# Turning u and spreading the S5 tables with SBUF-to-SBUF DMAs in a one-core S5 and sparse-attention trunk

## The chip, the core and the metric

The kernel runs on one core of a Trainium2 chip. The metric is the device time of one execution in microseconds (us), from the first to the last instruction and a little around it. Five engines work side by side, each in its own order of instructions: TensorE (PE, the matmuls; PEld are its weight loads), VectorE (DVE), ScalarE (ACT), GpSimd (POOL) and SyncE (SP, which issues nearly all loads here). SP, ACT and POOL can each issue DMAs, and all of these run on the core's 16 DMA engines.

## The reference, cut to what matters

The model is a two-layer decoder trunk on 256 positions of width 2048 in float32. Layer 0 is a diagonal state-space mixer (S5), layer 1 is sparse attention; between them one shared set of keys and values is projected. Every sub-layer is normalised and modulated by vectors that come from c (shift, scale, gate). Around the change only this part counts:

```python
u, z = jnp.split(h @ w_in, 2, axis=-1)
ug = u.reshape(B_, L, SSM_GROUPS, SSM_GROUP)          # 128 groups of 16 channels
bu = jnp.einsum('blgc,gnc->blgn', ug, bb)             # per group: 16 channels -> 64 states
x  = associative_scan(a, bu)                          # over the 256 positions, complex
y  = einsum('blgn,gcn->blgc', x, c) + d_skip * ug     # per group: 64 states -> 16 channels
y  = gelu(y); y = y * sigmoid(y @ w_glu + b_glu)
out = (y * silu(z)) @ w_out
```

The modulation vectors are products of silu(c) with large weights (`mod_w`, `kv_mod_w`); "a modulation block" below means 128 of their outputs, 1 MiB of weights.

## The kernel before, in words

All large projections are done block by block (128 output channels, 1 MiB of weights). A block is loaded in two halves of 512 KB into a ring of eight raw buffers (`raw_tile`, L95). `split_w` (L195) turns each raw buffer into a rounded part `hi` (ACT, L203) and a rest `lo` (DVE, L204), and `project_half` (L223) multiplies them with the activations in three matmuls for each of eight slices of 128 inputs (L228 to L230), 24 matmuls for a half. A raw buffer is free again when DVE is done with it, so a late DVE holds up the loads, which are issued in order on SP.

The modulation blocks are done in one of two ways. `dve_mod` (L138, "d") loads a block as two raw buffers and multiplies and sums each against silu(c) with one DVE instruction (L145). `pe_mod_pair` (L150, "m") does two blocks on TensorE (L158, L163). `NA` and `NB` (L40) say how many blocks go to TensorE: 18 here, with 78 on DVE.

u is projected in two parts. Its first eight blocks are computed row by row in `u_rows` (L289), while the normalised input h is still being made. The other eight blocks are "u" halves, and the sixteen blocks of z are "z" halves (`u_half` L567, `z_half` L578), which are placed by hand. `PLAN` (L59) is a list of strings, one for each call of `fill()` (L593): a letter is a half of u or z, a modulation block (d) or pair (m), or a piece of the later stages (c, q). Calls of `fill()` stand between the steps of the S5 scan, so the strings set which projection work stands beside which step. A scheduler in the compiler then orders each engine's instructions by its own estimate of when they are ready, with the order of the program as priority.

The S5 part works on two halves f of the groups (eight blocks each). For each of them:

- `u_out` (L544) evicts a block of u from PSUM into the tile x0. `u_turn(f)` (L547) then brings the channels of a group and four sub-sequences j of positions together on the partitions: for each of four g, eight matmuls with columns of a selection matrix `pick` (L556), and one eviction by ACT (L558).
- `scan_in(f)` (L598): 128 small matmuls of u with the input tables, evicted by ACT (L615, L616), with four calls of `fill()`.
- `scan_run(f)` (L627): the scan over time on DVE (L634 to L656).
- `scan_local(f)` (L658): the part of y that comes from the same short stretch of positions. Its tables (`kdt`, made at L485 to L491) are first spread into `tz`: for each of two g2 and two hl, four matmuls with a selection matrix `sel` (L668) and one eviction by ACT (L670). Then come the products tp (L676, weights from `tz`) and their eviction (L678), with one `fill()` for each g2.
- `scan_out(f)` (L681): the products of states and output tables (L692), added to U on DVE (L697), with two calls of `fill()`.
- `y_turn(f)` (L702): the way back to channels on partitions (L708), with gelu on the eviction (L711); then `y_split`.

The order is scan_in, scan_run and scan_local of half 0, two calls of `fill()`, u_turn(1), scan_in(1), scan_out(0), scan_run(1), scan_local(1), y_turn(0), y_split(0), `fill()`, scan_out(1), y_turn(1), y_split(1), `fill()`, and then the rest of z with the d's and m's of one string of the plan (L717 to L744). The glu projection (L747), w_out (L763), the norm, the projections for keys and values (w_kv) with the first rows of q, and the attention follow, with more strings. `q_rows` (L888) runs extra d's itself if the modulation blocks that a row of q needs have not been done yet (L899).

POOL issues few DMAs: the tables at the start, the row of silu(c) (`cact`, L534) and the second half's output tables (L624).

## Time and profile before

| what | value |
|---|---|
| time, median of three runs (lowest to highest) | 1359.1 us (1358.23 to 1368.98) |
| profiled execution, its own device time | 1356.18 us |
| its span, first to last instruction | 1354.5 us |
| mean granted TensorE clock | 0.971 |
| TensorE busy | 1267.1 us (94%) |
| VectorE busy | 1056.9 us (78%) |
| ScalarE busy | 688.1 us (51%) |
| GpSimd busy | 21.7 us (2%) |
| DMA traffic | 331.05 MB, mean 244 GB/s |

Busy time is the union of an engine's instructions, so matmuls that overlap count once. A granted clock of 1.0 is the higher of TensorE's two levels. The DMA share is the mean busy share of the 16 DMA engines in a stretch. "Idle before" is the time that an engine sat still just before a group's instructions, with what ended most of it.

### The profile page before, as it was taken

To read this page: it belongs to the slowest core of one execution; us is meant where nothing else is said; L and a number is where in the kernel's file an instruction comes from. 1 tells how busy PE (TensorE), PEld (TensorE's weight loads), DVE (VectorE), ACT (ScalarE), POOL (GpSimd) and SP (SyncE) were. 2 spreads that over 40 slices of the span, in tenths; PEclk is the share of its full clock that TensorE was granted. 3 is DMA by queue.
4 is the path that set the end of the run, shared out by engine and by line. 5 is a ranking of instruction groups with operands and counts; after the bars stand their busy time and mean duration, and the time that the engine had idled before them with its cause. 6 is when DMAs were issued, how large, how long until landed. Compare 5 with 4: busy or idle time off the path is not lost.

```text
span 1354.5 us, 31620 instructions
## 1 busy us (share of the span) xinstructions
PE 1267.1 (94%) x12526; PEld 1203.9 (89%) x12526; DVE 1056.9 (78%) x2291; ACT 688.1 (51%) x1463; POOL 21.7 (2%) x47
## 2 busy tenths in 40 slices
PE   2799999999889999998999899999999999999995
PEld 1678888888789999997999899999999999999995
DVE  5999769799768787659997878777888777776665
ACT  3345543437435555445455445555555565555653
POOL 2000000000100000000000000000000000000001
PEclk9899998999899999997999999999999999999998
DMA  9799954545879899869998789876555444444541
GB/s 342 259 384 316 350 194 147 212 138 197 295 280 362 299 344 327 309 232 385 322 352 272 241 278 326 273 253 216 175 199 192 149 154 145 154 143 154 187 157 62
DMA packets 93253, 331.05 MB, mean 244 GB/s; under 512 B 12512, under 2 KB 12672, under 8 KB 92080
## 3 DMA queue, kind: packets, MB, share of 16 engines
q1 hardware_dynamic: 91792, 321.45, 67.8%
q0 software_dynamic: 1312, 7.58, 1.5%
q8 instruction: 98, 1.61, 0.5%
q14 instruction: 51, 0.42, 0.1%
HBM read 324.79 MB, written 4.19 MB: 243 GB/s over the span
## 4 chain that ended last, share of the span: by engine, by line
PE 62%; DMA 4%; DVE 3%; issue 1%; ACT 1%; DVEq 0%; ACTq 0%
PE acc L230 18%; PE acc L229 18%; PE acc L228 18%; DMA raw<-in_mt_dram 3%; PE s L1002 1%; DVE lo L204 1%; PE op L1053 1%; PE macc L158 1%; PE op L1050 1%; DMA raw<-in_w_kv_dram 1%; DVE raw L145 1%; PE op L1054 1%; PE cp L838 0%; PE qacc L915 0%; PE cp L839 0%
## 5 line engine op out<-in xcount | busy, mean ns | idle before, releaser
L203 ACT ACTIVATE hi<-raw 128x512 fp32r<-128x512 f32 x640 | 400.0, 630 | 450.7 <-PE acc L229 388.6
L204 DVE TENSOR_TENSOR lo<-raw,hi 128x512 fp32r<-128x512 f32 x640 | 433.2, 688 | 154.5 <-ACT hi L203 148.2
L229 PE MATMUL acc<-hq,hi 128*128 128x256 f32 x960 | 274.6, 286 | 0.0
L228 PE MATMUL acc<-hq,hi 128*128 128x256 f32 x960 | 273.1, 285 | 0.4 <-ACT hi L203 0.4
L230 PE MATMUL acc<-hq,lo 128*128 128x256 f32 x960 | 271.0, 284 | 1.5 <-DVE lo L204 1.3
L145 DVE SCALAR_TENSOR_TENSOR raw<-raw,ey 128x1024 f32<-128x1024 f32 x156 | 189.9, 1220 | 63.0 <-DMA raw<-in_mt_dram 57.3
L229 PEld LDWEIGHTS acc<-hq,hi 128*128 128x128 f32 x960 | 181.0, 189 | 3.7 <-issue 3.3
L230 PEld LDWEIGHTS acc<-hq,lo 128*128 128x128 f32 x960 | 180.4, 189 | 3.5 <-DVE lo L204 2.1
L228 PEld LDWEIGHTS acc<-hq,hi 128*128 128x128 f32 x960 | 181.0, 189 | 1.2 <-issue 0.7
L230 PE MATMUL acc<-h,lo 128*128 128x256 f32 x384 | 112.3, 294 | 9.4 <-DVE lo L204 9.3
L230 PE MATMUL acc<-hkv,lo 128*128 128x256 f32 x384 | 112.3, 293 | 4.5 <-DVE lo L204 4.3
L228 PE MATMUL acc<-hkv,hi 128*128 128x256 f32 x384 | 112.0, 292 | 0.9 <-ACT hi L203 0.9
L228 PE MATMUL acc<-h,hi 128*128 128x256 f32 x384 | 112.8, 294 | 0.0
L229 PE MATMUL acc<-hkv,hi 128*128 128x256 f32 x384 | 111.0, 289 | 0.0
L229 PE MATMUL acc<-h,hi 128*128 128x256 f32 x384 | 110.2, 287 | 0.0
L230 PEld LDWEIGHTS acc<-h,lo 128*128 128x128 f32 x384 | 74.5, 195 | 12.4 <-DVE lo L204 11.4
L230 PEld LDWEIGHTS acc<-hkv,lo 128*128 128x128 f32 x384 | 76.1, 198 | 6.1 <-DVE lo L204 5.8
L158 PE MATMUL macc<-mraw,cz 128*32 128x128 f32 x1600 | 56.5, 292 | 24.4 <-DMA mraw<-in_m0n_dram 19.8
L228 PEld LDWEIGHTS acc<-hkv,hi 128*128 128x128 f32 x384 | 76.4, 199 | 1.5 <-ACT hi L203 1.5
L228 PEld LDWEIGHTS acc<-h,hi 128*128 128x128 f32 x384 | 74.6, 194 | 2.9 <-issue 0.8
L229 PEld LDWEIGHTS acc<-hkv,hi 128*128 128x128 f32 x384 | 76.4, 199 | 0.0
L229 PEld LDWEIGHTS acc<-h,hi 128*128 128x128 f32 x384 | 74.7, 195 | 0.0
(339 smaller groups left out, 2808.3 us busy)
## 6 DMA issues: line engine op xcount, KB each, us to landing
raw<-in_mt_dram SPq DMA_DIRECT2D x156, 512.0 KB, 5.8
raw<-in_w_z_dram SPq DMA_DIRECT2D x96, 512.0 KB, 3.8
mraw<-in_m0n_dram SPq DMA_DIRECT2D x64, 512.0 KB, 8.0
raw<-in_w_in_dram SPq DMA_DIRECT2D x48, 512.0 KB, 5.3
raw<-in_w_kv_dram SPq DMA_DIRECT2D x48, 512.0 KB, 6.2
mraw<-in_mn_dram SPq DMA_DIRECT2D x36, 512.0 KB, 6.1
raw<-in_w_glu_dram SPq DMA_DIRECT2D x32, 512.0 KB, 6.6
raw<-in_w_out_dram SPq DMA_DIRECT2D x32, 512.0 KB, 5.9
```

What stands on the lines that cost most here:

```text
L145: nc.vector.scalar_tensor_tensor(out=rf, in0=rf, scalar=1.0, in1=cact[:, 1024 * e:1024 * e + 1024], op0=OP.mult, op1=OP.mult, accum_out=mo ...
L158: nc.tensor.matmul(acc[32 * j:32 * j + 32, 128 * e:128 * e + 128], cz[:, q, :], r[:, q % 8, :], start=(e == 0 and q < 4), stop=(q >= 12), ...
L203: nc.scalar.activation(hi[:, 0:c, :], rr, AF.Copy)
L204: nc.vector.tensor_sub(lo[:, 0:c, :], rr, hi[:, 0:c, :].bitcast(F32))
L228: nc.tensor.matmul(acc, hi[:, kk, :], act(0, k), start=(k == 0), stop=False)
L229: nc.tensor.matmul(acc, hi[:, kk, :], act(1, k), start=False, stop=False)
L230: nc.tensor.matmul(acc, lo[:, kk, :], act(0, k), start=False, stop=(k == KT - 1))
L1002: nc.tensor.matmul(sp, qo(a, h)[:, qs], kk[:, kv, b, o:o + w], start=(i == 0), stop=(i == 2))
L1050: nc.tensor.matmul(op_, vc[0:15, kv, :], tcm[0:15, :], start=True, stop=True)
L1053: nc.tensor.matmul(op_, vt[:, kv, br - 1, 0, :], t[:, 0:256], start=True, stop=False)
L1054: nc.tensor.matmul(op_[:, 128:256], vt[:, kv, br - 1, 1, :], t[:, 256:384], start=False, stop=True)
```

## The change

u_turn becomes 32 DMAs for each half, each of 16 partitions with rows of 2 KB, half of them issued by ACT and half by POOL. The spread tables are written by DMAs from `kdt` into `tz`, in sets of 16 issued by POOL (`load_tz`), after `tz` has been set to zero once. The matrices `pick` and `sel` go, with their matmuls and evictions. U, the copy of u and the tables get an order of elements in which each DMA row is contiguous, so other steps read or write through other views, and the making of `kdt` has one ACT instruction more. TensorE gets 16 modulation blocks and DVE 80, and the plan is rewritten up to the keys and values: slot 0 now stands before scan_in(0), and a slot stands right behind u_turn(1).

```diff
-NA, NB = 10, 8
+NA, NB = 12, 4
 PLAN = [
-    "ud", "ud", "ud", "ud", "uu", "uu", "uuuud", "uuuudd", "zd", "z", "zd", "z", "z", "z", "zz", "zz",
-    "zz", "zz", "zz", "zz", "zz", "d", "d", "d", "", "d", "", "d", "zzzzzzddddddmm",
-    "d", "", "d", "d", "", "d", "d", "", "d", "d", "m", "d", "d", "", "d", "d",
-    "d", "m", "d", "", "d", "d", "", "m", "d", "", "d", "", "d", "", "", "",
-    "mmmm",
+    "uduudu", "u", "u", "u", "u", "uuuu", "uu", "uu", "zzzz", "z", "z", "z", "z", "z", "z", "zzzz", "zz",
+    "z", "z", "z", "z", "zz", "d", "d", "d", "", "d", "", "d", "zzzzddddm",
+    "d", "d", "d", "d", "m", "d", "d", "d", "d", "d", "m", "d", "d", "d", "d", "m",
+    "d", "d", "d", "d", "m", "d", "d", "d", "d", "m", "d", "d", "d", "", "d", "",
+    "mm",
     "d", "d", "d", "d", "dcd", "dc", "cd", "dcd", "cd", "cd", "cd",
...
-    kdt = [t.rearrange("p (m n) -> p m n", m=8) for t in kdt]
+    kdt = [t.rearrange("p (d n m) -> p d n m", d=4, m=8) for t in kdt]
...
-        nc.scalar.activation(kx, kp[:, :, 0], AF.Copy, scale=par[:, 0:1])
-        V.scalar_tensor_tensor(kx, in0=kp[:, :, 1], scalar=par[:, 1:2], in1=kx, op0=OP.mult, op1=OP.add)
+        nc.scalar.activation(kx, kp[:, :, 0].rearrange("p x (d c) -> p x d c", d=4), AF.Copy, scale=par[:, 0:1])
+        k1 = tk("k1").rearrange("p (x d c) -> p x d c", x=4, d=4)
+        nc.scalar.activation(k1, kp[:, :, 1].rearrange("p x (d c) -> p x d c", d=4), AF.Copy, scale=par[:, 1:2])
+        V.tensor_add(kx, kx, k1)
...
-    U = pool.tile([128, KT, 4, 64], F32, tag="uu", name="U")
+    U = pool.tile([128, 2, 4, 8, 64], F32, tag="uu", name="U")
...
+    nc.gpsimd.memset(tz, 0.0)
+
+    def load_tz(f, g2):
+        for hl in range(2):
+            for e in range(2):
+                i = 64 * g2 + 32 * hl + 16 * e
+                for j in range(4):
+                    o = 64 * e + 16 * j
+                    nc.gpsimd.dma_start(tz[o:o + 16, hl, j:4], kdt[f][i:i + 16, 0:4 - j])
     powers()
+    load_tz(0, 0)
     nc.gpsimd.dma_start(cact, crow.to_broadcast((128, D)))
...
         for g in range(4):
-            p = psb([128, 8, 64], "ut")
             for j in range(4):
                 for e in range(2):
-                    o = 64 * e + 32 * (j // 2)
-                    i = 32 * (2 * g + e) + (0 if j % 2 else 16)
-                    nc.tensor.matmul(p[o:o + 32].rearrange("p m (i s) -> p m i s", i=8), pick[:, i:i + 32], ucm[:, bs, :, j, :], start=(j % 2 == 0), stop=(j % 2 == 1),
-                                     skip_group_check=True)
-            nc.scalar.activation(U[:, bs, g, :], p, AF.Copy)
+                    o = 64 * e + 16 * j
+                    (nc.gpsimd if e else nc.scalar).dma_start(U[o:o + 16, f, g], ucm[f][32 * g + 16 * e:32 * g + 16 * e + 16, j])
...
         for g2 in range(2):
-            for hl in range(2):
-                pr = slice(64 * g2 + 32 * hl, 64 * g2 + 32 * hl + 32)
-                p = psb([128, 8, 4, 16], "tzp")
-                for j in range(4):
-                    nc.tensor.matmul(p[:, :, j:4, :], sel[pr, 48 - 16 * j:176 - 16 * j], kt[pr, :, 0:4 - j, :],
-                                     start=(j == 0), stop=(j == 3), skip_group_check=True)
-                nc.scalar.activation(tz[:, hl], p.rearrange("p m j c -> p m (j c)"), AF.Copy)
             for hl in range(2):
                 p = psb([128, 8, 64], "tp")
                 for m in range(8):
                     for e in range(2):
                         pr = slice(64 * e, 64 * e + 64)
-                        nc.tensor.matmul(p[pr, m, :], tz[pr, hl, m, :], U[pr, 8 * f + m, 2 * g2 + hl, :],
+                        nc.tensor.matmul(p[pr, m, :], tz[pr, hl].rearrange("p d n m -> p (d n) m")[:, :, m], U[pr, f, 2 * g2 + hl, m, :],
                                          start=(m == 0), stop=True, skip_group_check=True)
-                nc.scalar.activation(U[:, bs, 2 * g2 + hl, :], p, AF.Copy)
+                nc.scalar.activation(U[:, f, 2 * g2 + hl], p, AF.Copy)
+            if 2 * f + g2 < 3:
+                load_tz(f + g2, 1 - g2)
             fill()
...
+    fill()
     scan_in(0)
     scan_run(0)
     scan_local(0)
     fill()
-    fill()
     while ustate[0] < 2 * (16 - NR):
         u_half()
     u_turn(1)
+    fill()
     scan_in(1)
```

## Rows read from the trace of the kernel before

**Rows 1.** The page's first part: engine, busy us, share of the span, instructions.

```profile
PE 1267.1 (94%) x12526; PEld 1203.9 (89%) x12526; DVE 1056.9 (78%) x2291; ACT 688.1 (51%) x1463; POOL 21.7 (2%) x47
```

**Rows 2.** Stretches: S5 part, glu and w_out, keys and values, attention.

```profile
core 0: us, PE busy (x) PEld busy (x) DVE busy (x) ACT busy (x) POOL busy (x), PEclk, DMA share, GB/s
164.00:412.00 248.00, 234.50 (x3011) 207.81 (x3010) 200.97 (x367) 115.74 (x219) 4.64 (x15) 0.96 0.61 214
412.00:624.00 212.00, 205.44 (x2016) 200.23 (x2014) 160.56 (x300) 109.90 (x211) 0.00 (x0) 0.98 0.88 314
624.00:836.00 212.00, 202.85 (x1620) 198.69 (x1621) 181.74 (x362) 108.37 (x212) 0.00 (x0) 0.96 0.87 304
836.00:1247.00 411.00, 409.16 (x3315) 398.51 (x3314) 312.92 (x844) 226.64 (x559) 0.00 (x0) 1.00 0.56 189
```

**Rows 3.** Shorter stretches of the same view: glu, the last m's, keys and values.

```profile
412.00:507.00 95.00, 94.90 (x835) 94.06 (x834) 78.64 (x144) 52.89 (x99) 0.00 (x0) 1.00 0.92 331
605.00:624.00 19.00, 13.12 (x275) 9.99 (x273) 14.03 (x35) 9.71 (x26) 0.00 (x0) 0.82 0.89 323
624.00:730.00 106.00, 104.61 (x836) 102.05 (x837) 98.51 (x194) 55.47 (x104) 0.00 (x0) 0.95 0.94 341
730.00:836.00 106.00, 98.24 (x786) 96.64 (x785) 83.23 (x169) 52.91 (x108) 0.00 (x0) 0.97 0.79 266
```

**Rows 4.** Stretches, tile ut alone (PE, PEld, ACT busy): the two turns of u.

```profile
166.00:174.00 8.00, 7.10 (x64) 2.19 (x64) 2.32 (x4) 1.00 0.91 275
245.00:254.00 9.00, 7.10 (x64) 2.19 (x64) 2.38 (x4) 1.00 0.79 306
```

**Rows 5.** Stretches, tile tzp alone (PE, PEld, ACT busy): the tables' spread.

```profile
188.00:212.00 24.00, 8.06 (x32) 4.93 (x32) 2.39 (x4) 0.86 0.35 115
283.00:306.00 23.00, 8.06 (x32) 4.93 (x32) 2.39 (x4) 0.93 0.47 165
```

**Rows 6.** Timeline of PE (start us, us): two slices of a projection in steady state.

```profile
243.65 0.28 PE L228 MATMUL acc<-h,hi 128*128 128x256 f32 x1
...
244.01 0.28 PE L228 MATMUL acc<-h,hi 128*128 128x256 f32 x1
```

**Rows 7.** Timeline of POOL: issues of DMAs.

```profile
4.59 3.62 POOL L416 DMA_DIRECT2D stab<-in_dvec_dram  x4
...
282.32 1.06 POOL L624 DMA_DIRECT2D ct<-ctd  x2 [137.66 <-issue]
```

**Rows 8.** DMA issues: KB each, median us from issue to landing.

```profile
stab<-in_dvec_dram POOLq DMA_DIRECT2D x4, 2.0 KB, 13.2
...
l<-in_b2row_dram POOLq DMA_DIRECT2D x1, 0.5 KB, 1.7
```

**Rows 9.** Timeline of SP: one issue that waits for nothing.

```profile
163.15 0.33 SPq L191 DMA_DIRECT2D raw<-in_w_in_dram  x1
```

**Rows 10.** Timeline of DVE: the tables' end, scan_run(0)'s first and last, scan_run(1)'s first.

```profile
163.04 0.22 DVE L491 TENSOR_TENSOR ey<-ey,dg 128x64 f32<-128x64 f32 x1
...
187.90 0.69 DVE L634 TENSOR_TENSOR scr<-Vva,stab 128x512 f32<-128x512 f32 x1 [1.73 <-ACT Vva L615]
...
257.09 1.08 DVE L656 TENSOR_TENSOR Vva<-Vva,scr 128x896 f32<-128x896 f32 x1
...
269.43 0.69 DVE L634 TENSOR_TENSOR scr<-Vvb,stab 128x512 f32<-128x512 f32 x1 [1.72 <-ACT Vvb L615]
```

**Rows 11.** Timeline of ACT: the last eviction of y_turn(1).

```profile
366.28 0.60 ACT L711 ACTIVATE U<-yt 128x512 f32<-128x512 f32 x1 [0.35 <-PE yt L708]
```

**Rows 12.** Groups by line, 164 to 412 us: xcount, busy us, mean ns, idle before.

```profile
L676 PEld LDWEIGHTS tp<-U,scr 64*64 64x64 f32 x256 | 9.3, 156 | 0.8 <-issue 0.7
...
L558 ACT ACTIVATE U<-ut 128x512 f32<-128x512 f32 x8 | 4.8, 597 | 9.8 <-PE ut L556 9.8
```

**Rows 13.** The page's fifth part: a modulation half on DVE.

```profile
L145 DVE SCALAR_TENSOR_TENSOR raw<-raw,ey 128x1024 f32<-128x1024 f32 x156 | 189.9, 1220 | 63.0 <-DMA raw<-in_mt_dram 57.3
```

More of the change, by code (lines that the diff above doesn't have):

```diff
@@ L219, in split @@
     def split(act, k, src):
-        nc.scalar.activation(act(0, k), src, AF.Copy)
-        nc.vector.tensor_sub(act(1, k), src, act(0, k).bitcast(F32))
+        hi, lo = act(0, k), act(1, k)
+        if len(src.shape) == 3:
+            hi, lo = [t.rearrange("p (a b) -> p a b", a=src.shape[1]) for t in (hi, lo)]
+        nc.scalar.activation(hi, src, AF.Copy)
+        nc.vector.tensor_sub(lo, src, hi.bitcast(F32))
     def project_half(src, act, half, acc):
@@ L499, in trunk_kernel @@
             nc.scalar.activation(VH[:, :, hq_].rearrange("p r h b m -> p h r (b m)"), p, AF.Copy)
-    ucm = x0.rearrange("p m (i j s) -> p m i j s", i=8, j=4)
-    U = pool.tile([128, KT, 4, 64], F32, tag="uu", name="U")
+    ucm = [x0[:, 8 * f:8 * f + 8, :].rearrange("p a b -> p (a b)").rearrange("p (j m k) -> p j m k", j=4, m=8) for f in range(2)]
+    U = pool.tile([128, 2, 4, 8, 64], F32, tag="uu", name="U")
     scr = pool.tile([128, 4096], F32, tag="cb", name="scr")
@@ L511, in trunk_kernel @@
     w1, w2_ = [scr[:, 192 * i:192 * i + 192] for i in range(2)]
-    tz = scr[:, 2944:3968].rearrange("p (l m n) -> p l m n", l=2, m=8)
+    tz = scr[:, 2944:3968].rearrange("p (l d n m) -> p l d n m", l=2, d=4, m=8)
     def powers():
@@ L702, in y_turn @@
     def y_turn(f):
-        for mp in range(4 * f, 4 * f + 4):
+        for mp in range(4):
             p = psb([128, 2, 8, 4, 8], "yt")
@@ L714, in y_split @@
         for m in range(8 * f, 8 * f + 8):
-            split(yhl, m, ycm[:, m].rearrange("p j k -> p (j k)"))
+            split(yhl, m, ycm[:, f, :, m - 8 * f, :])
+    fill()
     scan_in(0)
```

30 lines of the change are left out of this document (11 added, 19 removed).

## The prediction

> **What bounds the kernel now.** I read the page's first part first: TensorE is busy 94% of the span and no other engine over 78% [rows 1]. Then I cut the span into stretches to see where that holds [rows 2]. In the S5 stretch (164 to 412 us) PE is busy 234.5 of 248 us while the DMA engines are at 0.61 and DVE at 201: time comes off here if PE's work does. From 412 to 836 us PE is busy 408 of 424 us, but the DMA engines stand at 0.88 and 0.87, and in single stretches at 0.92 and 0.94 with 331 and 341 GB/s [rows 2, 3]: PE and DMA are nearly level, and what is moved there can cost. The attention (836 to 1247 us) has its DMA engines at 0.56 and PE full; the change leaves its blocks alone, so I carry it over unchanged.
>
> **The change, part by part.** The sum is made against the profiled execution's own 1356.2 us (span 1354.5 and 1.7 around it); the median of the runs shown is 1359.1, so 2.9 is added at the end.
>
> *The turn of u.* Two turns, each 32 matmuls in 64 instructions, 7.10 us of PE each [rows 4]. PE is full in both places and the next step, scan_in, needs their result, so all of it was on the path: -14.2 us.
>
> *The spread of the tables.* Per half 16 matmuls in 32 instructions, 8.06 us of PE [rows 5], with DVE as full as PE around them. What makes me count them on PE: after the scan's last step PE still has z halves to do up to 412 us (chain, below). -16.1 us, so -30.3 with the turn.
>
> *What the DMAs cost.* A set of 16 on POOL: issues one behind the other took 1.06 us for two, 0.53 each [rows 7], so 8.5 us, and the last one's data come 1.7 us after its issue as for the small load there [rows 8]: 10.2 us. ACT's 16 issues at SP's 0.33 each take 5.3 us [rows 9]. What covers a set: four halves of a projection. Eight slices of three matmuls at 0.36 us a slice [rows 6] are 2.9 us for a half, 11.5 us for four. The plan puts "uuuu" behind load_tz(0,1), "zzzz" behind load_tz(1,1) and behind u_turn(1): 10.2 under 11.5, nothing exposed. load_tz(1,0) is issued some 50 us before its use. The first turn is different: POOL does load_tz(0,0) first, from the tables' end at 163.0 us [rows 10], so its share of the turn is issued from 171.5 to 180 and lands at 182, while slot 0's cover, begun at about 163, ends near 175. Exposed 7 us if PE waits, none if the scheduler brings the u's of slots 1 to 4 forward. I take +4. The bounds: 0, and with 0.9 us an issue and 13.2 to landing, as for the four small table loads whose rows are single elements [rows 7, 8], 27.7 us for a set; I stay with the nearer rows because every row here is 512 bytes or more.
>
> *ACT.* It loses 8 evictions of the turn [rows 12] and 8 like them of the spread, 9.6 us, and gains 32 issues at 0.33, 10.6 us, and four small ones for `kdt`. Busy 116 of 248 us [rows 2], so the exchange is hidden; a set of 5.3 us in front of the `hi` splits is about two halves, as long as the split buffers last. Taken as 0; without that cover up to 5 us for two turns.
>
> *Strided views.* The tp products load weights from every eighth element. No row shows such a load; the loads were busy 9.3 us for both halves [rows 12]. Between 0 and a doubling, +9; taken as 0, as in the contiguous row, since the number of loads and columns is the same. The views that ACT and DVE write through: 0, by the slack of both in rows 2.
>
> *Modulation blocks moved.* Counting the plan's letters, 20 blocks on DVE and 2 pairs on PE stood before the glu, now 11 and 1. So 7 more are loaded in glu, w_out and the "mm" behind them (16+11+2 block loads with weights, 16+7+4 and x, and 8, against 16+13+6, 16+12+4 and x, and 4), and 4 more with keys, values and q. At 1.05 MB a block: 314 GB/s times 212 us is 66.6 MB, with 7.3 more 73.9; at the 341 GB/s of the best stretch [rows 3] that takes 216.7 us, +4.7. One PE pair fewer (2.3 us of PE) stands in this stretch, where DMA sets the length, and counts nothing. For the four in the next stretch there is room in total (0.79 at its end, 22 us idle) but q_rows now has to force five d's in its last three rows, one before: 3.1 us each at 341 GB/s, 12 us for the four, if nothing covers; I take +3. Bounds: 0 and +12. DVE: 7 blocks at two times 1.22 us [rows 13], 17 us, leave the stretch of the first scan, 10 us into the last one, which had 30 us free.
>
> *TensorE's clock.* The granted clock is a mean of 0.86 where the spread of half 0 stands and 0.93 for half 1 [rows 5]: part of the time at the lower level. Work lost: 0.14 of 24 and 0.07 of 23 us, 5 us. It may come back with these matmuls gone, or a wait for a DMA may take as much. Taken as 0; bounds -5 and +5.
>
> *What is late next.* The chain scan_run(0), scan_run(1), y_turn(1). Before, scan_run(1) starts at 269.4, 12 us after scan_run(0)'s end at 257.1 [rows 10], because PE brings scan_in(1) late; y_turn(1) ends at 366.3 [rows 11], 46 us before the glu. Afterwards scan_in(1) stands behind 22 us less of PE's removed work, 11.5 us more z and the 4 us wait, so scan_run(1) starts near 263, while scan_run(0) without 17 us of d's would be done by 244. Then 97 us to y_turn(1)'s end, less 8.1 and two z halves (5.8), gives 346; the stretch's end, 412 - 30.3 + 4 = 386, less ten z halves and the 11 us that twelve of them took over their 35, needs it at 346. PE stays the bound, with nothing to spare.
>
> Sum: -30.3 + 4 + 4.7 + 3 = -18.6, so 1337.6 for a profiled execution and 1340.5 by the median: I say 1340.
>
> One rule weighed against this: the row for two issues shows 0.53 us each, one behind the other [rows 7]. The Trainium skill ("DMA: Bandwidth & Descriptors", Rules for kernel authors) says to merge small transfers, under 64 KB being mostly overhead, and its section on the path from GpSimd puts the fixed part at about 2.0 us for each. These DMAs have 32 KB at most; if each fixed part stood alone a set would take 33 us (an estimate from that page), 22 beyond its cover. The row speaks for overlapping issues; the rival that this rule describes is the first below.
>
> **The rivals.**
>
> *The sets come late (slower).* Each of the four covered sets (both turns, load_tz(0,1) and (1,1)) takes longer than its 11.5 us, and scan_in and the tp products wait with all that follows on PE. It decides from the point where the wait eats 30.3 - 7.7 = 22.6 us: 5.7 us a set, a set of 17 us, one us an issue. For it: table loads at 0.9 us and 13.2 us [rows 7, 8], ACT's and POOL's queues are in order, and loads of weights share the 16 engines. Against: 0.53 us an issue for two large transfers and 1.7 us to landing for a small one. At the price of 27.7 us a set: 16 us exposed four times, 65 - 22.6 = +42, 1401.
>
> *DMA fills later (within 1%).* Eleven blocks that stood beside a DMA at 0.61 go where it is near 0.9. At the glu's 331 GB/s the first stretch takes 223 us (+11), and the forced d's all show (+12): -30.3 + 4 + 11 + 12 = -3, 1356. For it: in the 19 us of the last m's PE is busy only 13 with DMA at 0.89 [rows 3]. Against: 7.3 MB is a tenth more in a stretch with an eighth idle.
>
> *The scan becomes the bound (within 1%).* If y_turn(1) still ends at 366, ten z halves and their 11 us end at 406: -6 in place of -26, then +7.7: 1361. For it: DVE's 201 of 248 us, and the chain above has no slack. Against: 17 us of d's leave it.
>
> *All of it comes back (faster still).* No wait, the clock's 5 us and the pair's 2.3 us: -37.6, 1321.5.
>
> **How the numbers follow.** A measurement of this kernel tells about 1%, 13.6 us, from no change: faster means under 1345.5. Forecast 0.47; all of it 0.11; DMA fills 0.16; the scan 0.09; late sets 0.17. So faster 0.58, same 0.25, slower 0.17. The range takes in the full gain and the two cases around no change: 1321 to 1362; beyond it lie most of the late sets and little below. The likeliest case's own range is 1328 to 1349 (below: without the turn's 4 and the forced 3, and with the clock's 5; above: all forced d's).
>
> **What would show it.** Right: no rows of ut and tzp; PE's busy sum near 1235 us; scan_run(1) starting near 263 and glu near 386 us; 96 DMAs on POOL at 0.5 us each; the stretch of glu and w_out a few us longer with DMA over 0.9. Wrong: PE idle over 5 us before vp or tp with a DMA as releaser (late sets); glu starting at 386 but keys and values not earlier than 615 (DMA fills); PE idle after scan_run with DVE as releaser (scan).

## The result, and the profile after

The changed kernel takes 1370.1 us (median of 13 runs, 1365.7 to 1373.3); the kernel before, run beside it, 1359.0 (13 runs). The ratio is 1.0075, 95% interval [1.0053, 1.0097]: slower, by less than the 1% that the prediction took as its bound. Forecast were 1340 us and a range of 1321 to 1362, so the measured time lies outside. The profiled execution after is 1371.4 us (span 1369.4, mean granted clock 0.962), before 1356.2 (1354.5, 0.971).

The page's first part after, which answers [rows 1]:

```profile
PE 1262.9 (92%) x12266; PEld 1211.3 (88%) x12266; DVE 1060.8 (77%) x2303; ACT 675.8 (49%) x1446; POOL 66.7 (5%) x139
```

TensorE lost 260 instructions and only 4.2 us of busy time. The same four stretches as in [rows 2], with the same columns:

```profile
164.00:412.00 248.00, 224.41 (x2832) 212.35 (x2823) 200.74 (x396) 113.97 (x213) 49.89 (x107) 0.94 0.62 208
412.00:624.00 212.00, 205.72 (x1992) 200.04 (x1991) 169.01 (x317) 105.81 (x208) 0.00 (x0) 0.98 0.92 345
624.00:836.00 212.00, 192.41 (x1441) 185.64 (x1441) 168.09 (x338) 96.13 (x185) 0.00 (x0) 0.91 0.79 266
836.00:1247.00 411.00, 411.00 (x3351) 401.70 (x3349) 322.60 (x866) 229.42 (x567) 0.00 (x0) 1.00 0.59 201
```

The third row is the surprise: between 624 and 836 us the clock fell from 0.96 to 0.91, PE's busy time by 10 us and the DMA share from 0.87 to 0.79. To place the loss I cut both executions at events instead of at times: the first matmul on `yhl` (the glu starts), the last on `ghl` (w_out ends), the last on `hkv` (keys and values end), the end.

| stretch | before, us | after, us | difference |
|---|---|---|---|
| start to glu | 412.3 | 398.2 | -14.1 |
| glu and w_out | 192.8 | 202.7 | +9.9 |
| end of w_out to end of keys/values | 224.3 | 244.2 | +19.9 |
| the rest | 525.1 | 524.3 | -0.8 |

The sum is +14.9, the difference of the spans. So the S5 stretch gained half of the 26 us that were forecast, and the two stretches behind it gave back twice that. In glu and w_out two pairs of modulation blocks more stand on TensorE now: 5.7 us of the +9.9 are their matmuls, and PE idles 2.4 us more (192.1 us busy of 192.8 before, 199.6 of 202.7 after). In return two pairs fewer stand at the junction (the "mm" between w_out and the norm of keys/values), and the first product on `hkv`, the normalised input of the keys and values, comes 209.5 us after the glu's start, against 211.7.

The groups of PE by line, 164 to 412 us, answer [rows 4, 5, 12]; there is no row of `ut` or `tzp` any more:

```profile
L670 PE MATMUL tp<-U,scr 64*64 64x64 f32 x256 | 17.5, 283 | 0.0
L612 PE MATMUL vp<-U,Vvb 64*64 64x64 f32 x256 | 10.6, 245 | 7.6 <-DMA U<-x 7.6
L612 PE MATMUL vp<-U,Vva 64*64 64x64 f32 x256 | 10.4, 236 | 5.3 <-DMA U<-x 4.7 <-ACT Vva L499 0.5
```

PE now waits for the turn's DMAs in both turns, and the local product `tp` is busy 17.5 us, where it was 9.8. The scans' first steps and the last eviction of y_turn(1), which answer [rows 10] and [rows 11] (timelines of DVE and ACT):

```profile
202.86 0.69 DVE L637 TENSOR_TENSOR scr<-Vva,stab 128x512 f32<-128x512 f32 x1 [1.72 <-ACT Vva L618]
...
278.73 0.69 DVE L637 TENSOR_TENSOR scr<-Vvb,stab 128x512 f32<-128x512 f32 x1 [1.73 <-ACT Vvb L618]
...
390.96 0.58 ACT L707 ACTIVATE U<-yt 128x512 f32<-128x512 f32 x1
```

All three are later than before. The DMAs into the tile `U` that ACT and POOL issue (duration of an issue min/median/max in ns, first and last start), then two rows of the DMA issues from 150 to 330 us (KB each, median us to landing); they answer [rows 7 to 9]:

```profile
L561 ACTq DMA_DIRECT2D U<-x x32: 514/600/1737, 159.9 to 248.1; - x32
...
L561 POOL DMA_DIRECT2D U<-x x32: 484/487/521, 160.2 to 245.5; - x32
```

```profile
U<-x ACTq DMA_DIRECT2D x32, 32.0 KB, 2.8
...
scr<-ey POOLq DMA_DIRECT2D x8, 32.0 KB, 2.9
```

An issue costs ACT 0.60 us, not the 0.33 of SP's row.

### The profile page after: what moved, and what is told of

It reads as the page before. It is cut to its first block, busy times and chain, and to the rows that moved or that the text cites. A ratio compares the mean times of both kernels' runs of the same rounds, so it can differ in the third digit from the quotient of the medians.

```text
span 1369.4 us, 31323 instructions
## 1 busy us (share of the span) xinstructions
PE 1262.9 (92%) x12266; PEld 1211.3 (88%) x12266; DVE 1060.8 (77%) x2303; ACT 675.8 (49%) x1446; POOL 66.7 (5%) x139
## 4 chain that ended last, share of the span: by engine, by line
PE 75%; DMA 10%; DVE 9%; issue 3%; ACT 2%; ACTq 1%; SPq 0%; DVEq 0%
PE acc L233 20%; PE acc L231 20%; PE acc L232 19%; DMA raw<-in_mt_dram 5%; DVE lo L204 2%; PE macc L158 2%; DMA mraw<-in_m0n_dram 2%; DVE raw L145 2%; PE s L1000 1%; PE tp L670 1%; PE vp L612 1%; PE op L1051 1%; DMA U<-x 1%; PE uacc L302 1%; ACTq L561 1%
## 5 line engine op out<-in xcount | busy, mean ns | idle before, releaser
L145 DVE SCALAR_TENSOR_TENSOR raw<-raw,ey 128x1024 f32<-128x1024 f32 x160 | 194.6, 1220 | 54.5 <-DMA raw<-in_mt_dram 51.9
L233 PE MATMUL acc<-hkv,lo 128*128 128x256 f32 x384 | 116.9, 305 | 11.0 <-DVE lo L204 10.9
L232 PE MATMUL acc<-hkv,hi 128*128 128x256 f32 x384 | 114.8, 300 | 4.9 <-DVE hkv L266 4.7
L231 PE MATMUL acc<-hkv,hi 128*128 128x256 f32 x384 | 115.2, 301 | 3.6 <-ACT hi L203 3.3
L233 PEld LDWEIGHTS acc<-hkv,lo 128*128 128x128 f32 x384 | 79.7, 208 | 14.2 <-DVE lo L204 13.8
L232 PEld LDWEIGHTS acc<-hkv,hi 128*128 128x128 f32 x384 | 79.4, 207 | 6.3 <-DVE hkv L266 6.3
L231 PEld LDWEIGHTS acc<-hkv,hi 128*128 128x128 f32 x384 | 79.4, 207 | 4.9 <-ACT hi L203 4.9
```

The source lines that it names most:

```text
L145: nc.vector.scalar_tensor_tensor(out=rf, in0=rf, scalar=1.0, in1=cact[:, 1024 * e:1024 * e + 1024], op0=OP.mult, op1=OP.mult, accum_out=mo ...
L231: nc.tensor.matmul(acc, hi[:, kk, :], act(0, k), start=(k == 0), stop=False)
L232: nc.tensor.matmul(acc, hi[:, kk, :], act(1, k), start=False, stop=False)
L233: nc.tensor.matmul(acc, lo[:, kk, :], act(0, k), start=False, stop=(k == KT - 1))
```

## The experiments

Eighteen kernels were run, in five groups. The letters are those of the plan. "Ratio" is to the kernel before, run on the same chip; beside the different groups its median was 1357.1 to 1362.6 us, so between kernels of different groups the ratio compares better than the medians. The last four columns come from one profiled execution each: the glu's start, then the two stretches of the table above, and "norm", from the first to the last of the 16 DVE instructions that write `hkv`. The expectations count keys/values from the first product on `hkv` to the last (205.4 us before, 237.4 after); the table begins at the end of w_out, so that the junction counts too. The one execution can lie some way from its kernel's median (e6: 1338.0 us against 1348.1), so a few us in these columns decide nothing. Every edit also lets the compiler order each engine's instructions anew; what this alone can do is seen at e11 and e15.

| kernel | median us (runs) | ratio, 95% | glu | glu, w_out | to end of k/v | norm |
|---|---|---|---|---|---|---|
| before | 1359.0 (13) | 1 | 412.3 | 192.8 | 224.3 | 16.8 |
| after | 1370.1 (13) | 1.0075 [1.0053, 1.0097] | 398.2 | 202.7 | 244.2 | 26.1 |
| e1 after, old blocks | 1376.8 (4) | 1.0115 [1.0082, 1.0148] | 419.0 | 200.0 | 229.3 | 16.5 |
| e2 before, new blocks | 1385.5 (4) | 1.0183 [1.0151, 1.0216] | 418.2 | 201.4 | 243.7 | 26.2 |
| e3 after, mmmm | 1356.5 (10) | 0.9965 [0.9943, 0.9988] | 391.4 | 205.1 | 224.4 | 11.6 |
| e13 after, mm twice | 1357.4 (10) | 0.9994 [0.9972, 1.0015] | 397.0 | 205.5 | 227.4 | 11.3 |
| e14 after, pairs early | 1382.1 (4) | 1.0182 [1.0129, 1.0235] | 397.7 | 214.3 | 240.8 | 26.1 |
| e17 after, d's later | 1362.2 (10) | 1.0016 [0.9988, 1.0044] | 397.5 | 203.5 | 231.3 | 16.2 |
| e12 after, turn on POOL | 1357.2 (10) | 0.9983 [0.9962, 1.0005] | 389.7 | 201.7 | 246.9 | 26.2 |
| e5 after, contiguous | 1374.5 (5) | 1.0106 [1.0074, 1.0139] | 394.5 | 204.7 | 242.4 | 26.2 |
| e4 e3, turn on POOL | 1343.1 (4) | 0.9873 [0.9835, 0.9910] | 390.3 | 201.5 | 224.7 | 10.8 |
| e6 e3, spread by DMA only | 1348.1 (6) | 0.9903 [0.9859, 0.9946] | 386.4 | 201.5 | 223.8 | 10.8 |
| e9 e6, contiguous | 1342.3 (4) | 0.9868 [0.9831, 0.9904] | 383.4 | 205.4 | 226.2 | 11.7 |
| e8 e3, contiguous | 1359.1 (10) | 0.9983 [0.9952, 1.0013] | 402.5 | 202.6 | 226.5 | 11.1 |
| e7 e8, turn by DMA only | 1378.4 (4) | 1.0132 [1.0090, 1.0175] | 424.1 | 200.5 | 225.7 | 10.8 |
| e10 e8, all matmuls | 1367.6 (10) | 1.0051 [1.0023, 1.0079] | 410.2 | 204.5 | 221.1 | 10.8 |
| e11 e4, contiguous | 1357.8 (10) | 0.9977 [0.9956, 0.9998] | 399.3 | 207.4 | 226.7 | 10.9 |
| e15 e11, turn first | 1342.4 (4) | 0.9900 [0.9842, 0.9958] | 386.3 | 201.9 | 225.5 | 10.8 |
| e16 e9, mmm | 1350.3 (10) | 0.9942 [0.9915, 0.9969] | 386.0 | 205.7 | 229.5 | 19.6 |
| e18 e15, mm, d's later | 1353.2 (10) | 0.9934 [0.9904, 0.9965] | 385.2 | 202.9 | 233.3 | 18.0 |

### The keys/values stretch: which part of the change loses the time

**e1**: the DMAs of the change with the old share of the blocks.

```diff
-NA, NB = 12, 4
+NA, NB = 10, 8
-    "zzzzddddm", ... "mm",
+    "zzzzddddddmm", ... "mmmm",
...
```

> The changed kernel (turn of u and spread by DMA) with the modulation blocks shared out as before: NA and NB back to 10 and 8, the slots from glu on as before (four pairs of blocks, mmmm, at the junction), and the nine d's of the S5 stretch back in it. Theory T1 (the junction and the loop of loads behind it set the keys/values loss): first keys/values product to first q product about 212 us again instead of 243, glu start near 398 as in the changed kernel, total 1335 to 1350. Rival T2 (the DMAs themselves, or the order that they bring, disturb keys/values): that stretch stays near 240 us, total 1365 to 1378. Rival T3 (S5 needs the DMA time that the nine d's take): glu starts later than 403, and the total comes out at 1350 to 1362.

Half of T1 came: keys/values takes 210.7 us. The total did not, because the glu starts at 419.0: nine `d`s and one pair back in S5 cost 21 us beside the DMAs of the turn. T3 had named that ("later than 403"), but far too small. The total, 1376.8, lies in T2's range, but T2's sign, a stretch near 240 us, did not come. Glu and w_out, with the blocks of before, take 200.0 us here and 192.8 in the kernel before, so part of the +9.9 above may not be the blocks'.

**e2**: the matmuls of before with the new share of the blocks.

```diff
-NA, NB = 10, 8
+NA, NB = 12, 4
-    "mmmm",
+    "mm",
...
```

> The kernel before (turn and spread by matmuls) with the changed kernel's share of the modulation blocks (NA and NB 12 and 4, two pairs at the junction, no d's in most of S5). T1: keys/values takes about 240 us and the total is 1375 to 1390, slower than both kernels, with glu start near 408 to 412. T2: keys/values stays near 212 us and the total is 1350 to 1362.

T1 holds: keys/values takes 237.0 us and the total, 1385.5, lies in its range (the glu starts later than it said, at 418.2). Without any of the DMAs the stretch from w_out's end is 243.7 us, and glu with w_out 201.4, both within 1.3 us of the changed kernel. So the loss belongs to the blocks that were moved, and on the same blocks the DMAs themselves are worth 15 us (1385.5 to 1370.1).

**e3**: the changed kernel with two more pairs at the junction.

```diff
-NA, NB = 12, 4
+NA, NB = 12, 8
-    "mm",
+    "mmmm",
```

> The changed kernel with two more pairs of blocks on TensorE at the junction (NB 8 instead of 4, mmmm for mm) and nothing else. T1: the junction is covered again as in rows 3, TensorE's idle time on the norm goes, and the later loop has four DVE blocks fewer to load: keys/values about 215 to 222 us with four more us of matmuls ahead of it, total 1345 to 1355. T2: keys/values stays near 240, total 1368 to 1378. A mixed case (junction mended, loop still at DMA's pace): 1358 to 1366.

Keys/values is at 204.7 us, better than T1 said, the stretch from w_out's end back at 224.4, and the kernel at 1356.5, 1.5 us above T1's range. But e3 does two things: two more pairs cover the junction, and DVE has four blocks fewer behind it. The next two take these apart.

**e13**: the junction's two pairs are computed twice, DVE's share stays.

```diff
-    "mm",
+    "mmnn",
...
+    def pe_again():
+        i = len(PE_MODS) - 4 + 2 * (len(again) - 1)
+        again.append(i)
+        pe_mod_pair((mn[i], mn[i + 1]), PE_MODS[i:i + 2])
```

> The changed kernel, in which the two pairs at the junction are computed twice (the same blocks, loaded again; about 13 us more of TensorE and 2 MB x 2 more of loads); DVE's share of blocks is as in the changed kernel. Theory J (the norm on DVE needs TensorE and the loads behind it covered for some 19 us): keys/values falls from 237 to 205 to 215 us and the total to 1354 to 1362 in spite of the extra work. Theory F (what counts is four blocks fewer for DVE and its loads): keys/values stays at 232 to 238, total 1378 to 1384.

**e14**: e3's four blocks fewer on DVE, with the two more pairs in glu and w_out.

```diff
-NA, NB = 12, 4
+NA, NB = 12, 8
-    "d",
+    "dm",
...
-    "d",
+    "dm",
```

> The changed kernel with NB 8 as in e3 (four blocks fewer on DVE), but mm at the junction as in the changed kernel: the two more pairs stand in glu and w_out (one each). Theory F: keys/values 205 to 212 us as in e3, total 1353 to 1360. Theory J: keys/values stays at 228 to 238, with 12 to 14 us more ahead of it, total 1376 to 1386.

Both go to theory J (keys/values 208.0 us in e13, 234.1 in e14). Work that is done twice makes the kernel 12.7 us faster (e13, 1357.4), and the same pairs put elsewhere make it 12 us slower (e14, 1382.1). The DVE instructions that write `hkv` (16 of them, first and last start) show what the cover does; the changed kernel, then e13, then e14:

```profile
L266 DVE SCALAR_TENSOR_TENSOR hkv<-xn,modv,hkv x16: 470/476/479, 607.7 to 633.8; 128x256 fp32r<-128x256 f32 x16
```

```profile
L272 DVE SCALAR_TENSOR_TENSOR hkv<-xn,modv,hkv x16: 475/480/485, 609.2 to 620.5; 128x256 fp32r<-128x256 f32 x16
```

```profile
L265 DVE SCALAR_TENSOR_TENSOR hkv<-xn,modv,hkv x16: 475/480/485, 618.7 to 644.8; 128x256 fp32r<-128x256 f32 x16
```

Each takes 0.48 us in all three, but their row is 26 us long in the changed kernel and in e14, and 11 in e13. What stands between them is in the timeline of DVE, the changed kernel first:

```profile
609.65 1.27 DVE L266 SCALAR_TENSOR_TENSOR hkv<-xn,modv,hkv 128x256 fp32r<-128x256 f32 x3
610.84 1.22 DVE L145 SCALAR_TENSOR_TENSOR raw<-raw,ey 128x1024 f32<-128x1024 f32 x1
...
618.17 1.22 DVE L145 SCALAR_TENSOR_TENSOR raw<-raw,ey 128x1024 f32<-128x1024 f32 x1
...
619.32 0.48 DVE L263 SCALAR_TENSOR_TENSOR xn<-x,scol,rstd 128x256 f32<-128x256 f32 x1
619.72 1.22 DVE L145 SCALAR_TENSOR_TENSOR raw<-raw,ey 128x1024 f32<-128x1024 f32 x1
```

```profile
618.92 0.47 DVE L272 SCALAR_TENSOR_TENSOR hkv<-xn,modv,hkv 128x256 fp32r<-128x256 f32 x1
619.32 0.47 DVE L269 SCALAR_TENSOR_TENSOR xn<-x,scol,rstd 128x256 f32<-128x256 f32 x1
619.71 1.27 DVE L272 SCALAR_TENSOR_TENSOR hkv<-xn,modv,hkv 128x256 fp32r<-128x256 f32 x3
...
624.25 1.22 DVE L144 SCALAR_TENSOR_TENSOR raw<-raw,ey 128x1024 f32<-128x1024 f32 x1
```

In the changed kernel eight halves of modulation blocks (1.22 us each) and ten `lo`s of the projections (0.68 us each) stand among the norm's slices, and PE, whose first products need a slice of `hkv` and a `lo` each, goes at DVE's pace (from 585 to 850 us it waits 4.7 us for `hkv` and 10.9 for `lo`). In e13 neither stands among them: the products begin when the norm is done, and the first half comes at 624.25, because behind the loads of the two extra pairs SP issues the first of the blocks' loads at 613.5 us, not at 603.7. What follows is in the stretches, with the columns of [rows 2]; the changed kernel, then e13:

```profile
608.00:640.00 32.00, 25.68 (x154) 23.48 (x154) 31.43 (x69) 16.07 (x36) 0.00 (x0) 0.79 0.85 307
640.00:680.00 40.00, 35.58 (x262) 34.85 (x262) 34.86 (x68) 16.34 (x29) 0.00 (x0) 0.87 0.85 290
680.00:720.00 40.00, 37.80 (x284) 37.48 (x283) 28.60 (x57) 19.35 (x35) 0.00 (x0) 0.87 0.81 266
720.00:760.00 40.00, 35.34 (x261) 32.27 (x261) 26.00 (x51) 16.14 (x36) 0.00 (x0) 0.91 0.66 211
```

```profile
622.00:640.00 18.00, 18.00 (x137) 18.00 (x137) 16.95 (x34) 8.65 (x18) 0.00 (x0) 0.89 1.03 404
640.00:680.00 40.00, 37.45 (x293) 37.05 (x293) 36.81 (x70) 18.16 (x32) 0.00 (x0) 0.91 0.90 311
680.00:720.00 40.00, 39.93 (x342) 39.82 (x341) 37.17 (x76) 22.81 (x42) 0.00 (x0) 1.00 0.94 341
720.00:760.00 40.00, 38.03 (x305) 35.38 (x305) 30.51 (x60) 21.19 (x44) 0.00 (x0) 1.00 0.80 253
```

From 608 to 640 us DVE is busy 31.4 of 32 us and PE 25.7, at a clock of 0.79: part of the time at the lower of its two levels. From then on the changed kernel is late: PE idles a little in every stretch, its clock stays under 1.0 up to 800 us, and from 640 to 760 us it takes its loads at 211 to 290 GB/s instead of 253 to 341. The slow 32 us alone do not explain this. The kernel before has them too, at its junction, with the same clock, and 0.96 in the next 40 us:

```profile
608.00:640.00 32.00, 25.73 (x309) 22.90 (x309) 28.58 (x64) 17.30 (x41) 0.00 (x0) 0.79 1.01 385
640.00:680.00 40.00, 39.08 (x317) 38.75 (x317) 38.44 (x74) 19.91 (x35) 0.00 (x0) 0.96 0.91 328
```

There PE does the pairs up to 624 us (309 matmul instructions in these 32 us, 154 in the changed kernel), and is busy 39.1 of the next 40.

**e17** asks whether the blocks among the norm's slices are the whole of it: the changed kernel with two pairs, the first four `d`s behind the junction moved to the end of keys/values.

```diff
-    "mm", "d", "d", "d", "d", ... "qq", "q", "q", "d", "d", "",
+    "mm", "", "", "", "", ... "dqq", "dq", "dq", "d", "d", "d",
```

> The changed kernel (two pairs at the junction, NB 4) with the d's of the first four slots behind the junction moved to the end of keys/values. If the DVE blocks among the norm's slices are the cost: the norm ends near 620 instead of 634, keys/values falls from 237 to 210 to 222 us, total 1350 to 1360. If it is the missing TensorE work that counts (an idle stretch, a lower clock and a late loop of loads behind it): keys/values 228 to 240, total 1364 to 1374.

In between (keys/values 224.6 us). The norm shortens from 26.1 to 16.2 us and the stretch from 244.2 to 231.3; but 9 of these 13 us are given back behind it (the rest grows from 524.3 to 533.3 in this execution, the slowest of its ten), and the total falls by 8 us, not by 13 as in e13. So the blocks among the slices are the larger part of the stretch's loss. Against e13 and e3 4 to 7 us of it remain. Nine `lo`s, 6.1 us of DVE, still stand among the norm's slices in e17; whether they are the rest was not tested.

### The S5 stretch: which of the two parts pays

**e12** and **e4**: in the changed kernel and in e3, POOL issues all DMAs of the turn.

```diff
-(nc.gpsimd if e else nc.scalar).dma_start(U[o:o + 16, f, g], ...)
+nc.gpsimd.dma_start(U[o:o + 16, f, g], ...)
```

> The changed kernel itself (two pairs at the junction, not e3's four), with one edit: all DMAs of the turn of u are issued by POOL. Theory A (ACT's time in issuing them is the cost): as from e3 to e4 (1356.5 to 1343.1), 8 to 14 us off 1370.1, so 1354 to 1362, while keys/values stays near 237 us. Rival: e4's gain hung on e3's order of blocks, and here the set on one queue comes late: 1366 to 1374.

> Base: e3 (changed kernel with mmmm at the junction, 1356.5 us, glu start at 391.4). All 32 DMAs of each turn of u are issued by POOL, none by ACT. Theory A (ACT, busy issuing its 16 DMAs, can't round the hi halves of the cover, so TensorE starves): ACT's 10 to 14 us of issue go, TensorE's wait ahead of vp on U falls although POOL needs 32 x 0.5 = 16 us a set, glu start 385 to 390, total 1350 to 1354. Rival B (what TensorE waits for is the set itself, whoever issues it): POOL's one queue makes each set later by 2 to 5 us, twice, and the first set pushes load_tz back too; glu start 394 to 402, total 1359 to 1368.

Theory A's totals came, for e4 by more than it said: 12.9 us off the changed kernel and 13.5 off e3, although POOL's queue now carries 32 issues a turn at 0.49 us. The timeline of ACT around the second turn, changed kernel first, then e12:

```profile
236.72 0.63 ACT L203 ACTIVATE hi<-raw 128x512 fp32r<-128x512 f32 x1 [0.79 <-PE acc L232]
237.26 0.36 ACT L552 ACTIVATE x<-acc 128x256 f32<-128x256 f32 x1
237.65 4.36 ACTq L561 DMA_DIRECT2D U<-x  x7
...
243.08 5.64 ACTq L561 DMA_DIRECT2D U<-x  x9
248.77 0.38 ACT L592 ACTIVATE x<-acc 128x256 f32<-128x256 f32 x1 [5.06 <-DMA U<-x]
249.05 2.18 ACT L203 ACTIVATE hi<-raw 128x512 fp32r<-128x512 f32 x4
```

```profile
237.66 0.63 ACT L203 ACTIVATE hi<-raw 128x512 fp32r<-128x512 f32 x1 [0.77 <-PE acc L232]
240.06 0.63 ACT L203 ACTIVATE hi<-raw 128x512 fp32r<-128x512 f32 x1 [1.77 <-PE acc L232]
241.49 0.63 ACT L203 ACTIVATE hi<-raw 128x512 fp32r<-128x512 f32 x1 [0.79 <-PE acc L232]
243.15 0.63 ACT L203 ACTIVATE hi<-raw 128x512 fp32r<-128x512 f32 x1 [1.03 <-PE acc L232]
```

In the changed kernel no `hi` is made between 237 and 249 us: the sixteen issues stand in front on ACT. The halves of projections that were to cover the set need a `hi` each, so the cover stops with the thing that it was to cover. The stretch from 240 to 260 us in the changed kernel, then in e12:

```profile
240.00:260.00 20.00, 12.39 (x115) 11.48 (x114) 18.78 (x31) 4.35 (x8) 5.56 (x12) 0.66 0.40 118
```

```profile
240.00:260.00 20.00, 20.00 (x225) 19.41 (x224) 19.20 (x45) 8.33 (x15) 5.29 (x12) 1.00 0.62 197
```

The Trainium skill ("DMA: Bandwidth & Descriptors", Issuing engines are not separate DMA queues) says that issuing from several engines saves only the issue time, usually small beside the DMA itself. In this kernel it was not small: sixteen issues kept ACT from 237.65 to 248.72 us, on the engine that also makes the operands.

Three things keep the 13 us from being the clean price of ACT's time. First, the edit also changed the compiler's order: in e12 the second set is issued from 215.8 us, not from 237.7, and the first `vp` behind it starts at 257.9, not at 243.6. So the set has long landed, and PE's 12.4 us of waiting for it are gone, but how much of the gain is the freed ACT and how much the earlier set is not separated. Second, the profiled executions of e3 and e4 do not show the gain where theory A puts it: their glu starts at 391.4 and 390.3. Third, the same one line is all that lies between e8 and e11 below, and there it takes away the wait (10.3 us) as well, but gives only 1.3 us (1359.1 to 1357.8).

**e6**, **e7**, **e9**, **e8**, **e10**: the two parts one by one, all with e3's blocks. In e6 and e9 the turn is by matmuls again, in e7 the spread, in e10 both; e9, e8, e7 and e10 have the tables in the order m, n of before, so that the weights of `tp` lie in one piece.

```diff
 # turn by matmuls (e6, e9, e10)
-                    (nc.gpsimd if e else nc.scalar).dma_start(U[o:o + 16, f, g], ...)
+                    nc.tensor.matmul(p[o:o + 32], pick[:, i:i + 32], ucm[f][:, j], ...)
+            nc.scalar.activation(U[:, f, g], p, AF.Copy)
 # spread by matmuls (e7, e10)
-                load_tz(f + g2, 1 - g2)
+                nc.tensor.matmul(p[:, :, j:4, :], sel[pr, 48 - 16 * j:176 - 16 * j], kt[pr, :, 0:4 - j, :], ...)
 # tables m, n (e5, e7 to e11, e15, e16, e18)
-tz = scr[:, 2944:3968].rearrange("p (l d n m) -> p l d n m", l=2, d=4, m=8)
+tz = scr[:, 2944:3968].rearrange("p (l m n) -> p l m n", l=2, m=8)
```

> Base: e3. The turn of u goes back to matmuls (2 x 32 of them, 14 us of TensorE by rows 4, and the evictions on ACT); only the spread of the tables is by DMA. Theory C (the turn by DMA gives back what it saves: 5 to 6 and 6 to 8 us of waiting ahead of vp and a lower clock against 14 us of matmuls): glu start within 5 us of e3's 391.4, total 1352 to 1361, and no wait of vp on U. Rival D (the turn by DMA carries half of the gain): glu start 400 to 406, total 1364 to 1371.

> Base: e3. The spread of the tables goes back to matmuls (2 x 16 of them for each of the two halves, 16 us of TensorE by rows 5), with the tables in the order m, n of before, so that the weights of tp are contiguous again (17.5 to about 10 us); only the turn of u is by DMA. Theory C: the spread's DMA is what pays; without it glu start goes from 391.4 to about 399 to 403 (+16 for the matmuls, -7.7 for the stride), total 1364 to 1370. Rival D: the turn's DMA pays as much as the spread's, so glu start is 391 to 396 and the total 1355 to 1360.

> Base: e6 (turn by matmuls, spread by DMA, mmmm), with the tables in the order m, n, so that the weights of tp are contiguous: tp 17.5 to about 10 us. If the stride costs what tp's busy time says, this is 5 to 8 us faster than e6, total 1346 to 1354, and it beats both kernels. Rival: TensorE has slack there, or the smaller rows of the spread make its sets late (landings of 3.3 to 5.1 us in e5 against 2.6): same as e6 within 3 us or slower.

> e3 with the tables in the order m, n (weights of tp contiguous), the turn still issued by ACT and POOL. If the stride costs TensorE what e6 to e9 shows (5.8 us), 1348 to 1353. Rival: with ACT busy issuing, TensorE starves anyway, and the time the stride gives back is spent waiting for the cover (as e5 against the changed kernel): 1355 to 1361.

> e7 with the turn of u by matmuls too: nothing by DMA, but the changed kernel's order of blocks with mmmm, tables m, n. With e9 (spread alone by DMA, 1342.3), e7 (turn alone, 1378.4) and e8 it makes a square of the two parts on one order. From e2 (1385.5) with mmmm's 13.5 us off: 1368 to 1375; then the spread's DMA is worth 26 to 33 us here and the turn's costs 3 to 10. Rival: the order matters little to the matmuls, and it is like the kernel before, 1355 to 1362; then the spread's DMA is worth 13 to 20 and the turn's costs 16 to 23.

With contiguous tables these make a square:

| median us | spread by matmuls | spread by DMA |
|---|---|---|
| turn by matmuls | 1367.6 (e10) | 1342.3 (e9) |
| turn by DMA, ACT and POOL | 1378.4 (e7) | 1359.1 (e8) |

The spread by DMA is worth 25.3 us beside the turn's matmuls and 19.3 beside its DMAs; the turn by DMA costs 10.8 and 16.8 (by the ratios 25 and 20, and 11 and 16). Theory C held in its direction, and the turn was worse than it said: e7's glu starts at 424.1 us, not at 399 to 403, and e6 and e9 are some 4 us under their ranges. So the change was one good part and one that cost, as it was issued. With POOL alone issuing, the turn by DMA is no loss in two of three kernels (e4 1343.1 beside e6's 1348.1, e15 1342.4 beside e9's 1342.3, but e11 1357.8). From e10 to e9 PE is busy 22.8 us less up to the glu, 6.7 more than the 16.1 us of the tables' matmuls, and the mean clock there goes from 0.95 to 0.99. From e7 to e8, beside the turn's DMAs, PE is busy 16.5 us less and the clock is 0.92 in both.

**e5** and the stride: with contiguous weights the loads of `tp` take 135 ns instead of 213 (tile `tp`, the changed kernel, then e9).

```profile
L670 PEld LDWEIGHTS tp<-U,scr x256: 192/213/216, 204.7 to 320.7; 64*64 64x64 f32 x128
L670 PE MATMUL tp<-U,scr x256: 280/280/330, 204.7 to 320.8; 64*64 64x64 f32 x128
```

```profile
L676 PEld LDWEIGHTS tp<-U,scr x256: 128/135/136, 201.1 to 304.7; 64*64 64x64 f32 x128
L676 PE MATMUL tp<-U,scr x256: 217/218/268, 201.1 to 304.8; 64*64 64x64 f32 x128
```

> The changed kernel with the tables kept in the order m, n of before, so that the weights of the local product (tp) lie in one piece; the spread's DMAs then move rows of 64 to 256 bytes, eight a partition. Stride theory: the tp group's busy time falls from 17.5 to about 10 us, weight loads from 213 to 135 ns, glu start about 7 us earlier, total 1361 to 1366. Rival (small rows make the sets of the spread late): landings grow from 2.6 to 5 us or more, TensorE waits ahead of tp, total 1368 to 1380.

The first half of the stride theory holds (`tp` 9.6 us of PE in e5, 9.4 in e9, not 17.5). The total does not follow: e5 is not faster than the changed kernel, nor e8 than e3. The rival's late sets are not the reason, as PE does not wait ahead of `tp` in e5; it waits 7.3 us for one `hi` and 8.6 for `lo`s, where the changed kernel waits 0 and 4.0, and in e8 it is 8.7 for one `hi`. That is what e8's rival said: the time goes into waiting for the cover. Only with the turn by matmuls did it go down, from 1348.1 (e6) to 1342.3 (e9), with intervals that overlap.

**e11** and **e15**: with POOL alone, contiguous tables made it worse (1343.1 to 1357.8), outside both ranges that I gave for e11. The timeline of POOL in e11 shows the first spread ahead of the turn, where e4 had the turn first (from 161.4 us):

```profile
166.37 4.26 POOL L539 DMA_DIRECT2D scr<-ey  x8 [18.97 <-issue]
...
177.50 0.51 POOL L558 DMA_DIRECT2D U<-x  x1 [0.55 <-issue]
```

e15 puts the spread behind the turn in the code.

```diff
-    load_tz(0, 0)
...
             u_turn(0)
+            load_tz(0, 0)
```

> e4 with the tables in the order m, n: both transposes by DMA, the turn issued by POOL alone, contiguous weights, mmmm. Both costs gone: 1335 to 1340, the best of all. Rival: in e4 the scan on DVE already sets the end of S5 (TensorE idle 260 to 300 on DVE), or POOL's queue is now late with the small rows: 1342 to 1350.

> e11 (both parts by DMA, the turn by POOL alone, contiguous weights; 1357.8) with the first spread's 16 DMAs issued behind the first turn's 32 instead of ahead of them. In e11 POOL issued the spread first (166 to 177), so the turn came 11 us later and the first vp at 199.7 instead of 175.3. If that order is what ate the gain: first vp near 175 again, total 1338 to 1346. Rival (the tables m, n cost elsewhere, in DVE's multiply-add for kx or in small rows): 1352 to 1358 again.

The total came (1342.4), but not by the sign that I gave: the first `vp` starts at 194.0 us in e15, against 199.7 in e11 and 175.3 in e4, and POOL's timeline in e15 still has the spread first:

```profile
163.75 4.23 POOL L539 DMA_DIRECT2D scr<-ey  x8 [18.40 <-issue]
...
174.23 1.93 POOL L557 DMA_DIRECT2D U<-x  x4 [0.72 <-issue]
```

The order in the code moved the turn by 3 us only. e15 is 15 us faster than e11 by the medians and 10 by the ratios. In the profiled executions the difference stands between 280 and 320 us, e11 first:

```profile
280.00:320.00 40.00, 21.59 (x299) 20.26 (x296) 31.24 (x49) 4.61 (x8) 9.49 (x18) 0.63 0.45 154
```

```profile
280.00:320.00 40.00, 31.33 (x365) 29.08 (x366) 39.17 (x78) 14.23 (x27) 9.43 (x18) 0.78 0.48 166
```

In e11 SP issues ten halves of modulation blocks in a row from 268.9 to 319.5 us and no half of z between them, so PE runs out of projections and waits 10.0 us for the next `lo`. In e15 seven halves of z are issued from 241.3 to 299.5 us, and the ten of the modulation blocks from 304.1. So the compiler put the loads in another order; why this edit turned it is open.

### Two more versions

**e16** is e9 with three pairs at the junction, **e18** is e15 with two pairs and e17's later `d`s.

> e9 (spread by DMA, turn by matmuls, contiguous weights, mmmm: 1342.3) with three pairs at the junction (NB 6). If three pairs, some 13 us of matmuls, still cover the norm: 1335 to 1340. If four are needed: keys/values grows from 206 to 215 to 230 and the total to 1345 to 1360.

> e15 (both parts by DMA, turn by POOL ahead of the spread, contiguous weights: 1342.4) with two pairs at the junction (NB 4) and the d's moved as in e17 instead of four pairs. If the moved blocks do the same as the two more pairs, 12 us of matmuls go: 1332 to 1340, the best of all. If not: 1350 to 1360.

Neither is better. With three pairs the norm takes 19.6 us and the stretch 229.5; with two and the `d`s away 18.0 and 233.3, and again the rest is longer (529.7 after 525.2). The best versions are e9, e15 and e4, at 1342.3, 1342.4 and 1343.1 us and 1.0 to 1.3% under the kernel before; their intervals overlap. Both forecasts had named this as the other outcome: e16 and e18 lie in the ranges given for it.

## Why the prediction was wrong

**Removed matmuls, -30.3.** Right: the rows of `ut` and `tzp` are gone. What came of it up to the glu was -14.1, where -26 was forecast. PE's busy sum did not come near 1235 us (1262.9): `tp` takes 7.7 us more, and the products on `hkv`, at the lower clock, 11.6 more.

**A set on POOL, 10.2 us.** Right for the tables: 0.49 us an issue and 2.2 to 3.2 us to landing, and PE never waited ahead of `tp`. For the turns the sign of the late sets came (PE idle 5.3 and 7.6 us ahead of `vp`, most of it on a DMA), and the rival was half right: the second turn's set took some 14 us, from ACT's first issue at 237.65 to the last one's end at 248.72 and 2.8 more to landing, over the 11.5 of its cover, though not at the one us an issue that the rival gave. The prediction set the Trainium skill's rule for merging small transfers ("DMA: Bandwidth & Descriptors", Rules for kernel authors) against its own sum, with an estimate of 33 us a set; the trace does not bear the estimate out, as the issues on POOL followed each other at 0.49 us.

**The first turn, +4.** PE waited 5.3 us there. The size was near by luck: POOL issued its share of the turn ahead of the tables, from 160 us, so the reason given for the +4 was not there.

**ACT, "the exchange is hidden", 0, and the cover of the second turn.** These failed, as one: I priced ACT's issues at SP's 0.33 us (measured: 0.60) and compared busy times, where the question was what stands behind the issues on ACT. The `hi` of the cover stood there. PE waited 7.6 us at the second turn and ran the 20 us around it at a clock of 0.66; e12, which takes the issues from ACT, is 12.9 us faster (with the reserve above on what else it changed). I had written that the cover holds "as long as the split buffers last" and did not follow it up.

**Strided views, 0.** `tp` costs 7.7 us more of PE, within the bound of +9 that I had set and near its end. Undoing it brought nothing while the turn was by DMA.

**Modulation blocks: glu and w_out with the junction, +4.7.** Came as -2.2. DMA ran at 345 GB/s, near the 341 that I took, but I let the pairs count for nothing. I also had one pair fewer in this stretch; in fact it has seven before and after, and the one fewer stands ahead of the glu. Two of the seven moved from the junction into glu and w_out. The junction got 12.1 us shorter (w_out's end to the first product on `hkv`: 18.9 us, then 6.8), 6 us a pair where I had priced one at 2.3, and glu with w_out 9.9 longer.

**Modulation blocks: keys, values and q, +3.** This is the step that sank the forecast. From the first product on `hkv` to the last it came as +32 (205.4 to 237.4 us), and +19.9 with the junction ahead of it. "There is room in total" was true and beside the point: I counted loads and the forced `d`s at the end, and read the 19 us of the last m's [rows 3] only as a place where DMA is at 0.89. They were the cover under which DVE's norm ran. With half of the cover the products on `hkv` started with the norm's first slice, and `d`s and `lo`s came in among the others: the norm took 26.1 us instead of 16.8, and PE went at its pace. None of the rivals had this mechanism; the signs that I gave for "DMA fills later" (glu at 386, keys and values after 615) did not appear either (398 and 608).

**The chain.** With the waits, scan_run(1) started at 279 us (forecast 263) and y_turn(1) ended at 391 (forecast 346), 7 us before the glu where it had been 46; "nothing to spare" was right. The sign of the scan's rival was small: PE waited 1.6 us for the scan's sums.

**The clock, 0 (bounds 5 either way, for the S5 stretch).** It went down: 0.96 to 0.94 there, and 0.96 to 0.91 in keys/values, for which I had no term. With the spread alone (e9) it is at 0.99 up to the glu.

The misses sum up against -18.6: 12.2 in S5 (8.9 more waiting at the turns than the +4, and 7.7 for `tp`, less about 3 for the pair that stands there no more), -6.9 up to keys/values, 29 in them, -0.8 in the rest, 33.5 in all; -18.6 and 33.5 give the +14.9 of the spans.
